# High and low parts of W_in's later pieces and of W_out, and the low part of o, made in halves of 512 columns

## The chip, the cores and the metric

The kernel runs on one core of one Trainium2 chip. The metric is the device time of one execution in microseconds, lower being better. One more execution was taken with the hardware profiler, and all views are of that one. Each engine (TensorE for matmuls, VectorE, ScalarE, GpSimd, and SyncE, which issues most transfers) runs its own instructions in the order in which the program lists them, and waits on semaphores where an instruction needs another engine's result.

## What is computed

One decoder block on 1024 tokens of 1024 features, in float32. An adaptive pre-norm feeds one input projection to 2304 columns. Eight heads of mixer A (window 128, two key heads, a sink logit) and eight heads of mixer B (a mixture of three dilated windows) attend. Each mixer's output is normed, the two are concatenated, and one output projection follows; then come a post-norm, a gate and the residual. The second half is a squared-ReLU MLP of 4096 features with the same frame.

```python
h = rms_norm(x, g_attn_pre) * (1 + sc_a) + sh_a
proj = h @ w_in                                   # 1024 x 2304
...
oa = banded_attention(qa, ka, va, A_WINDOW - 1, sink=sink_a)
ob = dilated_mixture_attention(qb, kb, vb)
mixed = concatenate([rms_norm(oa, g_mix_a), rms_norm(ob, g_mix_b)])
x = x + gt_a * rms_norm(mixed @ w_out, g_attn_post)
h = rms_norm(x, g_mlp_pre) * (1 + sc_m) + sh_m
x = x + gt_m * rms_norm(square(relu(h @ w_up)) @ w_down, g_mlp_post)
```

## The kernel before

**High and low parts.** Matmuls run on a format (fp32r) that keeps fewer bits than float32. To keep the accuracy, an operand is split: ScalarE writes a rounded copy, the high part, and VectorE subtracts it from the original and so writes the low part. A product takes three matmuls: high by high, high by low, low by high. The splitting is the work that the change touches, in three places.

**W_in** (`split_w`, lines 547 to 565) arrives as 18 pieces of 128 by 1024 in a staging ring of three slots. Each piece is split into a tile of a ring of three. ScalarE's `hi` is on line 557, VectorE's `lo` on line 560. The function has a parameter `parts`: pieces 0 to 3, which the first projection unit uses, are split in two parts of 512 columns each; pieces 4 to 17 (lines 1071 to 1073) are split whole. The projection's matmuls are on lines 979 to 983 (`chunk_mm`) and, for values, on lines 1054 to 1056 (`proj_v`).

**W_out** (`load_wo`, from line 1487) is split into eight chunks of 128 by 1024, multiplied by a column of norm gains on the way: ScalarE on line 1514, VectorE on line 1517. The result goes into the tile `hw`, which holds the projection's input until then, so a chunk of W_out must wait until the last projection unit has read two chunks of `hw` (`e_free`).

**o**, attention's output, is read back from memory for each block of 128 tokens (`load_o` in `out_block`). ScalarE's high part is on line 1645, VectorE's low part on line 1649; ScalarE then squares it in place (line 1653), VectorE adds the squares up (1657, 1658), a small matmul and GpSimd (1677) make the norm `rab`, and the products on lines 1698 to 1700 use both parts. For blocks 2 to 7 these tiles have 1024 columns, for blocks 0 and 1 they come as two tiles of 512.

**Attention's small steps** share the engines with all this from about 90 us to 415 us: scores (line 1265 for mixer B, 1319 for A), a masked minimum on VectorE (1283), the exponential on ScalarE (1290), a reciprocal (1293), a scaling on GpSimd (1295), transposes on TensorE (1369 to 1376), the high and low part of the probabilities `ph` (ScalarE 1383, VectorE 1387), and the product with the values (1399 to 1410).

**Who sets the order.** The program is not written out by hand. A list scheduler (`Sched`, lines 197 to 333) holds a queue of steps for each engine, each with a modelled duration, dependencies, ring slots that it takes and gives, and a priority number. It picks, again and again, the step with the earliest possible start; on one engine ties are broken by the lower priority number and then by the earlier made step (line 290). A step that depends on another one is ready a modelled latency after it, 0.14 us between ScalarE, VectorE and themselves (`lat`, line 128). TensorE has streams (projection and MLP are `dense`) among which a list of preferences decides. All instructions are then emitted in the order found. Steps of W_in have priority 0, those of W_out 4, those of o 2, the evacuations of the projection -1, and attention's steps 0 and 1.

The durations in the model are formulas, for instance for VectorE and for ScalarE from on-chip memory:

```python
def t_sb(n):
    return 0.098 + 0.00083 * n
...
def t_dv(n):
    return 0.066 + 0.00104 * n
```

**The MLP** follows from about 480 us to the end: seven products for each of eight half-steps (a scheme with sums and differences of sub-blocks), with its own splitting on lines 1913 to 1922, which the change leaves alone.

## Time and profile before

| what | value |
|---|---|
| three runs, us | 1112.59, 1112.41, 1110.45 |
| median, us | 1112.41 |
| the profiled execution's own time, us | 1111.34 |
| its span, first to last instruction, us | 1109.6 |
| TensorE busy, us | 1091.4 |
| VectorE busy, us | 832.9 |
| ScalarE busy, us | 653.2 |
| GpSimd busy, us | 182.1 |
| mean granted TensorE clock | 0.998 |

A line of the profile's groups reads: source line, engine, operation, tile written and tiles read, shapes, count, then total busy time and mean duration, then the idle time of the engine before these instructions and what ended it. PE is TensorE, PEld its loading of weights, DVE VectorE, ACT ScalarE, POOL GpSimd and SPq SyncE's queue of transfers. In a view in order of time, a line begins with the start and the duration in us. In the chain of waits a line is a piece of the one chain of work that ended last, followed back from the end of the program.

### The profile page before, as it was taken

The numbers are of one execution on the slowest core, as the hardware profiler recorded it, in microseconds if no ns is written. First come the engines' busy times: TensorE is split into PE (matmuls) and PEld (weight loads), VectorE is DVE, ScalarE is ACT, GpSimd is POOL, SyncE is SP. The second block draws the span as 40 slices with busy tenths as digits, with TensorE's granted clock in tenths as the row PEclk, the third lists the DMA queues.
The fourth block names the chain that finished last, engine by engine and source line by source line (L and its number), as shares of the span: only waits on it lengthen the run. The fifth ranks groups of instructions, "written<-read, shape, count | busy, mean of one in ns | idle before, by whom it ended". The sixth has DMA issues, their size and how long they took to land.

```text
span 1109.6 us, 15904 instructions
## 1 busy us (share of the span) xinstructions
PE 1091.4 (98%) x5538; PEld 920.2 (83%) x5538; DVE 832.9 (75%) x1472; ACT 653.2 (59%) x1159; POOL 182.1 (16%) x229
## 2 busy tenths in 40 slices
PE   8999999999999999999999999999999999999997
PEld 7898888888988878888888888888888888888885
DVE  8955777898788877789698653898644996527997
ACT  7745766888877766687675234743145632347544
POOL 3013344555632321110000000000000000000003
PEclk9999999999999999999999999999999999999999
DMA  9866758768636526546841379511578013583006
GB/s 362 288 216 197 208 149 248 205 206 242 169 123 206 155 66 229 190 176 227 333 176 39 114 256 345 167 58 52 193 268 313 18 58 114 190 324 132 1 1 152
DMA packets 97432, 198.65 MB, mean 179 GB/s; under 512 B 8328, under 2 KB 31432, under 8 KB 97352
## 3 DMA queue, kind: packets, MB, share of 16 engines
q1 hardware_dynamic: 96632, 195.43, 52.4%
q0 software_dynamic: 576, 2.10, 1.0%
q8 instruction: 44, 0.72, 0.3%
q14 instruction: 36, 0.29, 0.1%
q10 hardware_dynamic: 144, 0.11, 0.0%
HBM read 155.46 MB, written 42.14 MB: 178 GB/s over the span
## 4 chain that ended last, share of the span: by engine, by line
PE 84%; DVE 8%; ACT 3%; issue 2%; DMA 1%; POOL 1%; SPq 0%; POOLq 0%; DVEq 0%; ACTq 0%
PE mlp_ps L2156 18%; PE mlp_ps L2155 18%; PE mlp_ps L2154 18%; PE s_ps L1265 2%; PE pj L979 2%; PE pj L983 2%; PE pj L981 2%; PE y_ps L1698 2%; PE y_ps L1700 2%; PE y_ps L1699 2%; PE pj L1054 1%; PE pj L1056 1%; PE acc L979 1%; PE pj L1055 1%; PE o_ps L1399 1%
## 5 line engine op out<-in xcount | busy, mean ns | idle before, releaser
L2154 PE MATMUL mlp_ps<-hw 128*128 128x512 f32 x896 | 349.6, 390 | 0.0
L2155 PE MATMUL mlp_ps<-hw 128*128 128x512 f32 x896 | 348.7, 389 | 0.6 <-DVE hw L1919 0.6
L2156 PE MATMUL mlp_ps<-hw 128*128 128x512 f32 x896 | 348.6, 389 | 0.0
L2155 PEld LDWEIGHTS mlp_ps<-hw 128*128 128x128 f32 x896 | 168.2, 188 | 36.4 <-DVE hw L1919 1.0
L2154 PEld LDWEIGHTS mlp_ps<-hw 128*128 128x128 f32 x896 | 168.2, 188 | 35.2 <-issue 0.5
L2156 PEld LDWEIGHTS mlp_ps<-hw 128*128 128x128 f32 x896 | 168.2, 188 | 34.9
L1922 DVE TENSOR_TENSOR hw<-w,hw 128x1024 fp32r<-128x1024 f32 x94 | 111.6, 1220 | 106.7 <-ACT hw L1915 106.5
L1915 ACT CAST hw<-w 128x1024 fp32r<-128x1024 f32 x94 | 95.1, 1048 | 136.8 <-PE mlp_ps L2156 98.2
L2260 POOL TENSOR_TENSOR st<-st,nhalf 128x1 f32<-128x1 f32 x8 | 7.4, 927 | 596.6 <-DVE st L2257 596.5
L1915 ACT CAST hw<-u 128x1024 fp32r<-128x1024 f32 x48 | 48.7, 1051 | 64.6 <-PE mlp_ps L2156 64.6
L1387 DVE TENSOR_TENSOR ph<-pt_ps,ph 128x512 fp32r<-128x512 f32 (+1 forms) x110 | 69.3, 644 | 19.2 <-ACT ph L1383 18.4
L1295 POOL TENSOR_SCALAR p_sb<-p_sb,den 128x128 f32<-128x128 f32 (+3 forms) x64 | 52.6, 826 | 120.2 <-DVE den L1293 97.0
L1383 ACT CAST ph<-pt_ps 128x512 fp32r<-128x512 f32 (+1 forms) x110 | 59.1, 554 | 18.8 <-PE pt_ps L1372 17.3
L1922 DVE TENSOR_TENSOR hw<-u,hw 128x1024 fp32r<-128x1024 f32 x48 | 57.0, 1219 | 16.7 <-ACT hw L1915 16.7
L979 PE MATMUL pj<-hw,w_hl 128*128 128x512 f32 x160 | 68.1, 425 | 0.0
L2212 DVE TENSOR_TENSOR yacc<-yacc,mlp_ps 128x512 f32<-128x512 f32 x96 | 62.5, 682 | 7.1 <-PE mlp_ps L2156 7.0
L983 PE MATMUL pj<-hw,w_hl 128*128 128x512 f32 x160 | 63.2, 395 | 0.0
L981 PE MATMUL pj<-hw,w_hl 128*128 128x512 f32 x160 | 63.0, 393 | 0.0
L1157 POOL TENSOR_TENSOR ada_acc<-ada_acc,wa_st 128x512 f32<-128x512 f32 x42 | 55.0, 1310 | 46.2 <-ACT wa_st L1150 22.4
L1290 ACT ACTIVATE p_sb<-p_sb,mn 128x128 f32<-128x128 f32 (+3 forms) x64 | 49.7, 777 | 21.9 <-DVE mn L1283 20.1
L1265 PE MATMUL s_ps<-kt,qt 128*128 128x512 f32 (+2 forms) x192 | 48.8, 354 | 0.9 <-DVE mn L1283 0.7
L1698 PE MATMUL y_ps<-hw,oh 128*128 128x512 f32 x120 | 48.6, 405 | 1.0 <-DVE mn L1283 0.9
(219 smaller groups left out, 2097.4 us busy)
## 6 DMA issues: line engine op xcount, KB each, us to landing
hw<-s_dram SPq DMA_DIRECT2D x84, 512.0 KB, 4.4
wa_st<-in_w_ada SPq DMA_DIRECT2D x32, 512.0 KB, 5.3
w<-in_w_up SPq DMA_DIRECT2D x32, 512.0 KB, 5.1
w<-in_w_down SPq DMA_DIRECT2D x32, 512.0 KB, 8.3
s_dram<-hw SPq DMA_DIRECT2D x28, 512.0 KB, 4.5
qk_dram<-hl SPq DMA_DIRECT2D x52, 256.0 KB, 3.5
kt<-qk_dram SPq DMA_DIRECT2D x40, 256.0 KB, 5.8
w_st<-in_w_in SPq DMA_DIRECT2D x18, 512.0 KB, 4.4
```

The lines of the kernel that those rows point to most:

```text
L979: T.matmul(ps, wt[:, 0, c0:c0 + P], hw[:, k, 0, t], start=(k == 0), stop=False)
L981: T.matmul(ps, wt[:, 1, c0:c0 + P], hw[:, k, 0, t], start=False, stop=False)
L983: T.matmul(ps, wt[:, 0, c0:c0 + P], hw[:, k, 1, t], start=False, stop=(k == KC - 1))
L1265: T.matmul(s[:, :cw], q_t[u, h, qb // 4][:, qb % 4 * P:qb % 4 * P + P], k_t[u, h, m][:, hl, :cw], start=(hl == 0), stop=(hl == 1))
L1387: V.tensor_tensor(b["ph"][:, 1, :w], b["pt"][:, :w], b["ph"][:, 0, :w].bitcast(F32), ALU.subtract)
L1698: T.matmul(ps[:], oh, wh, start=(k == 4 * i), stop=False)
L1915: A.copy(out[j][0], flat(src[j]))
L1922: V.tensor_tensor(out[j][1], flat(src[j]), out[j][0].bitcast(F32), ALU.subtract)
L2154: T.matmul(ps[m][:], sh, mh, start=starts and k == 0, stop=False, **kw)
L2155: T.matmul(ps[m][:], sh, ml_, start=False, stop=False, **kw)
L2156: T.matmul(ps[m][:], sl, mh, start=False, stop=k == 3, **kw)
L2212: e = op("DVE", t_dv(512), lambda: V.tensor_tensor(y(), y(), ps[m][:], ALU.add), [e, ml.e_y[tb, n]], gives=gives, prio=1)
```

## The change

The loop over the later pieces of W_in asks for two parts. For W_out the two steps of each chunk become two steps for each half of 512 columns: a half waits only for the one chunk of `hw` that it overwrites, the second half's steps come after the first's on each engine, and the staging slot is given back after the last one. The event on which products wait is that of the second half. For o the low part alone is made in halves of four sub-blocks of 128 where the tile has 1024 columns; the squares and the products wait for the last one.

```diff
     for i in range(4, 18):
         load_w(i)
-        split_w(i, prio=0)
+        split_w(i, 2, prio=0)
...
-                def f_h(k=k, g=g, raw=raw):
-                    A.mul(wo_at(k, 0), raw().rearrange("p (n c) -> p n c", n=2), g)
-
-                def f_lo(k=k, g=g, raw=raw):
-                    V.scalar_tensor_tensor(wo_at(k, 1), raw().rearrange("p (n c) -> p n c", n=2), g, wo_at(k, 0).bitcast(F32),
-                                           ALU.mult, ALU.subtract)
-                eh = op("ACT", t_sb(D) + AP_COST, f_h, [es[i]] + [e_free[k // 4][x] for x in (2 * (k % 4), 2 * (k % 4) + 1)],
-                        prio=4)
-                ph2.e_wo[k] = op("DVE", t_dv(D) + AP_DV, f_lo, [eh] + turn + ([last_hl] if k > 3 else []), prio=4,
-                                 gives=[(r_stg, 1)] if j == 1 else [(r_w, 1), (r_wl, 1)] if k == 1 else [])
+                for n in range(2):
+                    def f_h(k=k, n=n, g=g, raw=raw):
+                        A.mul(wo_at(k, 0)[:, n], raw()[:, 512 * n:512 * n + 512], g)
+
+                    def f_lo(k=k, n=n, g=g, raw=raw):
+                        V.scalar_tensor_tensor(wo_at(k, 1)[:, n], raw()[:, 512 * n:512 * n + 512], g,
+                                               wo_at(k, 0)[:, n].bitcast(F32), ALU.mult, ALU.subtract)
+                    eh = op("ACT", t_sb(512) + AP_COST, f_h, [es[i], e_free[k // 4][2 * (k % 4) + n]] + ([eh] if n else []),
+                            prio=4)
+                    ph2.e_wo[k] = op("DVE", t_dv(512) + AP_DV, f_lo,
+                                     [eh] + turn + ([last_hl] if k > 3 else []) + ([ph2.e_wo[k]] if n else []), prio=4,
+                                     gives=[] if not n else [(r_stg, 1)] if j == 1 else [(r_w, 1), (r_wl, 1)] if k == 1
+                                     else [])
...
-            def f_ol():
-                V.tensor_tensor(b["hl", m][1], b["now", m], b["hl", m][0].bitcast(F32), ALU.subtract)
-            eo = op("DVE", t_dv(P * n), f_ol, [eh], prio=2)
+            eo = eh
+            for x in range(max(1, n // 4)):
+                def f_ol(x=slice(4 * x, 4 * x + 4)):
+                    V.tensor_tensor(b["hl", m][1][:, x], b["now", m][:, x], b["hl", m][0][:, x].bitcast(F32), ALU.subtract)
+                eo = op("DVE", t_dv(P * min(n, 4)), f_ol, [eh, eo], prio=2)
```

## The prediction

> **What bounds the kernel now.** I read the page's busy times first, then the table of stretches, then the chain of waits, and last the order of time around the places where TensorE lost time.

> ```profile
> span 1109.6 us, 15904 instructions
> PE 1091.4 (98%) x5538; PEld 920.2 (83%) x5538; DVE 832.9 (75%) x1472; ACT 653.2 (59%) x1159; POOL 182.1 (16%) x229
> ```

> The span and 1.7 us around it make the profiled execution's 1111.34 us; the other three runs have a median of 1112.41, and I take every difference off that median. TensorE is busy for 98% of the span, so a change that leaves its matmuls alone can win only from the 18.2 us in which it idles, and from little delays that its modelled ends hide. The change touches work between 50 and 475 us. The stretches that hold the most of it (from and to, length, then busy time and instructions of TensorE, weight load, VectorE, ScalarE and GpSimd, then clock, DMA share and GB/s):

> ```profile
> 100.00:150.00 50.00, 49.21 (x285) 40.82 (x284) 37.42 (x97) 34.93 (x75) 21.40 (x22) 1.00 0.65 180
> 150.00:200.00 50.00, 49.58 (x289) 42.45 (x287) 38.90 (x98) 33.71 (x66) 21.88 (x22) 1.00 0.66 203
> 200.00:250.00 50.00, 49.65 (x304) 43.00 (x303) 44.90 (x140) 41.50 (x121) 27.12 (x42) 1.00 0.69 203
> 300.00:350.00 50.00, 49.72 (x316) 44.20 (x315) 41.27 (x101) 33.30 (x68) 15.62 (x16) 1.00 0.50 151
> 350.00:400.00 50.00, 48.23 (x298) 41.27 (x297) 39.98 (x113) 37.03 (x79) 16.51 (x20) 1.00 0.47 140
> 400.00:450.00 50.00, 48.64 (x250) 40.22 (x250) 36.70 (x69) 32.17 (x52) 10.40 (x13) 1.00 0.53 175
> ```

> TensorE's idle time in these six is 0.79 + 0.42 + 0.35 + 0.28 + 1.77 + 1.36 = 4.97 us. VectorE is at 73% to 90% and ScalarE at 64% to 83%: on the mean neither is full, yet TensorE waits. What a wait is made of is seen in the chain, where whole low and high parts of weights stand ahead of attention's small steps:

> ```profile
> 99.26 1.14 DVE w_hl L560
> 115.31 1.24 DVE w_hl L560
> 160.55 1.24 DVE w_hl L560
> 227.26 1.14 DVE w_hl L560
> 328.58 1.20 DVE hw L1517
> 350.49 1.77 ACT hw L1514 x2
> 354.07 0.99 ACT hw L1514
> ```

> These lines (start, us, engine and line) are the low part of W_in (L560), the low part of W_out (L1517) and its high part (L1514). Each is followed within a few microseconds, 13 in one case, by a stall of TensorE. In order of time, one matmul row before each stall and one after:

> ```profile
> 102.72 0.38 PE L1399 MATMUL o_ps<-ph,v_hl 128*128 128x256 f32 x1
> 103.45 0.39 PE L1399 MATMUL o_ps<-ph,v_hl 128*128 128x256 f32 x1 [0.34 <-DVE ph L1387]
> ...
> 118.46 0.89 PE L1399 MATMUL o_ps<-ph,v_hl 128*128 128x256 f32 x2
> 119.18 0.40 PE L1404 MATMUL o_ps<-ph,v_hl 128*128 128x256 f32 x2
> ...
> 165.38 0.34 PE L1402 MATMUL o_ps<-ph,v_hl 128*128 128x128 f32 x2
> 165.99 0.97 PE L1265 MATMUL s_ps<-kt,qt 128*128 128x512 f32 x4 [0.28 <-DVE mn L1283]
> ...
> 239.98 0.40 PE L1410 MATMUL o_ps<-ph,va_hl 128*128 128x512 f32 x1
> 240.72 0.51 PE L1410 MATMUL o_ps<-ph,va_hl 128*128 128x512 f32 x1 [0.35 <-DVE ph L1387]
> ...
> 356.62 0.38 PE L1372 MATMUL pt_ps<-head,p_sb 128*128 128x128 f32 x2
> 357.93 0.38 PE L1399 MATMUL o_ps<-ph,v_hl 128*128 128x256 f32 x1 [0.92 <-ACT ph L1383]
> 358.65 0.39 PE L1399 MATMUL o_ps<-ph,v_hl 128*128 128x256 f32 x1 [0.34 <-DVE ph L1387]
> 358.88 0.39 PE L1404 MATMUL o_ps<-ph,v_hl 128*128 128x256 f32 x2
> 359.11 0.53 PE L1399 MATMUL o_ps<-ph,v_hl 128*128 128x256 f32 x2
> ```

> From start to start, two undisturbed matmuls of 256 columns take 0.23 us (358.88 to 359.11), so one takes 0.12, one of 512 twice that and one of 128 half. The rows' own durations are longer because a matmul's end overlaps the next one; an idle time in brackets therefore understates a loss. By starts, TensorE lost 0.73 - 0.12 = 0.61 us at 102.7; 0.72 - 0.23 = 0.49 at 118.5; 0.61 - 0.12 = 0.49 at 165.4; 0.74 - 0.23 = 0.51 at 240; and 0.72 - 0.12 = 0.60 at 357.9, with 0.92 of idle time ahead of it. That is 3.62 us, with a whole high or low part in the chain ahead of each.

> **The change, part by part.** It removes nothing from the arithmetic. It turns 14 whole pieces of W_in, 8 of W_out and 6 low parts of o into two instructions each: 28 more on VectorE (14 + 8 + 6) and 22 more on ScalarE (14 + 8), since o's high part stays whole. Their costs:

> ```profile
> 38.43 0.69 DVE L560 TENSOR_TENSOR w_hl<-w_st,w_hl 128x512 fp32r<-128x512 f32 x1
> 39.03 1.22 DVE L722 TENSOR_TENSOR hw<-xnT,hw 128x1024 fp32r<-128x1024 f32 x1
> ...
> 53.52 1.22 DVE L560 TENSOR_TENSOR w_hl<-w_st,w_hl 128x1024 fp32r<-128x1024 f32 x1
> 54.66 1.22 DVE L722 TENSOR_TENSOR hw<-full,hw 128x1024 fp32r<-128x1024 f32 x1
> ...
> 330.23 2.19 ACT L1514 ACTIVATE hw<-wo_st,head 128x1024 fp32r<-128x1024 f32 x2
> ...
> 103.76 1.33 ACT L1150 ACTIVATE wa_st<-wa_st,cond 128x512 f32<-128x512 f32 x2
> ...
> L1514 ACT ACTIVATE hw<-wo_st,head 128x1024 fp32r<-128x1024 f32 x8 | 9.0, 1156 | 2.6 <-PE pj L981 2.6
> L1150 ACT ACTIVATE wa_st<-wa_st,cond 128x512 f32<-128x512 f32 x42 | 29.6, 721 | 0.2 <-DMA wa_st<-in_w_ada 0.2
> L557 ACT CAST w_hl<-w_st 128x1024 fp32r<-128x1024 f32 x14 | 14.7, 1050 | 6.6 <-PE acc L983 4.0 <-DMA w_st<-in_w_in 1.4 <-PE pj L1056 1.0
> ```

> The first rows are the most useful, as the kernel already makes W_in's first pieces in halves. Durations alone would say 2 x 0.69 - 1.22 = 0.16 us more per piece. But the engine takes its next instruction before the last one's end: a half holds VectorE for 0.60 us (38.43 to 39.03), a whole for 1.14 (53.52 to 54.66). A split costs 0.06 us, and an instruction that is ready behind a weight waits at most 0.60 instead of 1.14: 0.54 less. On ScalarE a whole of W_out holds it for 2.19 - 1.16 = 1.03 us and a scaled half, taken from L1150, for 1.33 - 0.72 = 0.61, so a split costs 0.19 and shortens the queue by 0.42. W_in's casts (1050 ns whole, in the last row) I bound by the same 0.61 and 0.19.

> [...]

> By rows the added work is 28 x 0.06 = 1.7 us on VectorE and at most 22 x 0.19 = 4.2 us on ScalarE, over the 425 us from 50 to 475. I put it at nothing on the path, because the idle shares above hide it; where that cover is gone it is a rival.

> *W_in.* The high half is done after 0.61 us, so VectorE starts 0.44 us sooner. The last low half would end 0.61 + 0.60 + 0.69 = 1.90 us after the first cast starts, against 1.05 + 1.22 = 2.27 now, if nothing comes between: the staging slot, and with it the next load, comes free up to 0.4 us sooner, or later by what overtakes. No stall above is one of a projection matmul, so neither shows.

> *Overtaking.* The order is decided by the planner inside the program. It takes the earliest possible start, then the lower priority number, then the earlier made step. It adds 0.14 us between dependent steps even on one engine, so that after a first half any step that is already ready goes ahead of the second, even where the second half has the better number. On VectorE the second half must wait for the second cast besides. A step of priority 0 that ties with a ready second half of W_in loses, as W_in's steps were made first. W_out (priority 4) loses against all of attention (0 and 1).

> *Sum of the gain.* At the four VectorE places the cap is the smaller of 0.54 and the loss: 0.54 + 0.49 + 0.49 + 0.51 = 2.03. At 357 us three whole copies of W_out stand ahead on ScalarE; 3 x 0.42 = 1.26 of the 1.52 lost there. Upper end 3.3 us. Lower end: nothing, if the second half always follows at once. I take two thirds, 2.2 us, since the planner's 0.14 us lets a ready step past at most of these boundaries, and ties go the other way at some. 1112.4 - 2.2 = 1110.2.

> *W_out's earlier start.* Each half now waits for one chunk of hw to be free, not two. The row of L1514 has 2.6 us of idle that a projection matmul ended. A copy could start there one projection step sooner (three matmuls of 512 columns, 3 x 0.23 = 0.7 us), but no stall above waits for it; I take nothing, with 0.7 either way as the bound.

> *o's low part.* The products and the squares still wait for its last half: 0.06 us later, more if overtaken. That is the first rival.

> **The rivals.** *Slower: o's second half is overtaken.* It has priority 2, below nearly all of VectorE's other steps of that stage. The last block is the place:

> ```profile
> 473.74 1.22 DVE L1649 TENSOR_TENSOR ol<-o_sb,oh 128x1024 fp32r<-128x1024 f32 x1
> ...
> 478.97 1.68 POOL rab L1677
> ...
> 512.24 0.50 PE L2155 MATMUL mlp_ps<-hw 128*128 128x512 f32 x1 [0.55 <-DVE hw L1919]
> ```

> Low part, sum of squares and norm follow each other there, and the chain runs from that norm through ScalarE and VectorE to TensorE's stall at 512. A step of 1024 columns let in between costs 1.14 + 0.06 = 1.2 us, and with no spare time all of it reaches that stall. It decides the sign if it happens in the last block and in two of the five earlier ones without cover while the gain fails: 3 x 1.2 = 3.6, so 1116.0. Against it: in every row of stalls above it is attention that TensorE waits for, never o's low part.

> *No change.* The second halves follow at once, or what they let past is late for another reason; the added 1.7 us lies in idle time or, at worst, on the path: 1112.4 to 1114.1. For it: at 118.5 us the projection's rotation also stands between the weight and the step that TensorE waits for.

> *Faster still.* The planner's new order also mends stalls that I didn't list: up to all 4.97 us of idle time, 1107.4. For it: every later step moves, and VectorE's spare time is there. Against it: a new order makes new stalls as easily.

> That the halves aren't made is not a case: the loops are plain.

> **How the numbers follow.** A measurement of this kernel can tell about 0.2%, 2.2 us, from no change: faster is below 1110.2, slower above 1114.6. The forecast has 0.50 and sits on the bound, so half of it is faster and half the same. Faster still has 0.17, no change 0.15 (all within), slower 0.18. Faster 0.25 + 0.17 = 0.42; same 0.25 + 0.15 = 0.40; slower 0.18. The range takes in the forecast's ends (1109.1 to 1112.4), no change to 1114.1, most of faster still and the lower part of slower: 1107.0 to 1115.0. The likeliest case's own range is 1109.1 to 1112.4.

> **What would show it.** Right: on each of the two engines 28 more rows of 512 columns for W_in's later pieces and 16 for W_out, on VectorE 12 more for o, all of 0.60 to 0.80 us; attention's steps between halves on VectorE; the whole pieces gone from the chain; TensorE's idle time from 100 to 450 us down by a microsecond or more, and fewer waits for ph. Wrong: halves back to back with the stalls at the same steps (no change); a wait for ol or for rab before y_ps, or a longer one at the first MLP products (slower); stalls at quite other steps (the new order, not the halves, decides).

## The result, and the profile after

| what | before | after |
|---|---|---|
| median of six runs, us | 1111.14 | 1116.31 |
| lowest to highest, us | 1110.29 to 1112.59 | 1114.08 to 1120.38 |
| the profiled execution's own time, us | 1111.34 | 1114.08 |
| mean granted TensorE clock of the runs | 0.998 (profiled) | 0.994 to 0.998, mean 0.9963 |

The kernel became slower: the ratio is 1.005, with a 95% interval of 1.0036 to 1.0063, where 1110.2 us and most likely a small gain had been forecast. 1116.31 lies above the range, too. The forecast was counted from the median of the first three runs (1112.41), which is 1.3 us above the median of all six. The top of the page after:

```profile
span 1112.3 us, 15974 instructions
PE 1091.5 (98%) x5538; PEld 920.6 (83%) x5538; DVE 841.0 (76%) x1502; ACT 656.4 (59%) x1181; POOL 181.2 (16%) x227
```

TensorE's work is the same (1091.5 us against 1091.4), so all that was lost is idle time of TensorE or a lower clock. VectorE's busy time rose by 8.1 us. The prediction counted 1.7 us, by the time for which an instruction holds its engine (28 x 0.06), and full durations would make 4.5 (28 x 0.16), so some instructions also became longer. In the table of stretches (columns as in the prediction), first one row of the kernel before that was not shown:

```profile
250.00:300.00 50.00, 50.00 (x356) 46.13 (x355) 41.11 (x146) 43.06 (x123) 29.92 (x47) 1.00 0.77 219
```

Then the kernel after:

```profile
100.00:150.00 50.00, 49.21 (x291) 42.26 (x292) 38.61 (x101) 35.35 (x78) 21.89 (x22) 1.00 0.59 175
150.00:200.00 50.00, 49.28 (x280) 41.21 (x279) 39.74 (x101) 33.42 (x69) 21.69 (x22) 1.00 0.66 202
200.00:250.00 50.00, 49.00 (x297) 42.24 (x296) 43.76 (x141) 39.81 (x119) 27.46 (x41) 1.00 0.67 203
250.00:300.00 50.00, 49.28 (x340) 44.36 (x340) 44.90 (x144) 43.61 (x124) 28.47 (x45) 1.00 0.76 214
300.00:350.00 50.00, 49.52 (x320) 44.48 (x320) 39.33 (x106) 34.35 (x75) 17.16 (x18) 1.00 0.46 141
350.00:400.00 50.00, 46.97 (x286) 39.69 (x285) 44.68 (x124) 39.74 (x84) 15.75 (x19) 1.00 0.51 151
400.00:450.00 50.00, 49.49 (x264) 42.21 (x264) 35.52 (x68) 32.27 (x55) 9.91 (x14) 1.00 0.50 166
```

TensorE's idle time in these seven was 4.97 us before (1.77 of it from 350 to 400) and is 0.79 + 0.72 + 1.00 + 0.72 + 0.48 + 3.03 + 0.51 = 7.25 us. It grew in each stretch from 150 to 400 us and shrank only after that. The groups show the instructions that the change made:

```profile
L560 DVE TENSOR_TENSOR w_hl<-w_st,w_hl 128x512 fp32r<-128x512 f32 x36 | 26.9, 758 | 6.6 <-ACT w_hl L557 6.5
L557 ACT CAST w_hl<-w_st 128x512 fp32r<-128x512 f32 x36 | 21.6, 616 | 7.1 <-PE acc L983 4.0 <-DMA w_st<-in_w_in 1.9 <-PE pj L1056 1.0
L1518 DVE SCALAR_TENSOR_TENSOR hw<-wo_st,head,hw 128x512 fp32r<-128x512 f32 x16 | 11.5, 743 | 0.0
L1654 DVE TENSOR_TENSOR ol<-o_sb,oh 128x512 fp32r<-128x512 f32 x15 | 10.6, 721 | 0.3 <-ACT oh L1648 0.3
```

All halves were made. But a half of W_in on VectorE has a mean of 758 ns where the eight halves of the kernel before had 687. One of them, of 1.69 us, carries 1.0 us of the 2.6 us by which the 36 exceed that mean. In order of time, VectorE, GpSimd and TensorE around 205 us of the kernel after:

```profile
203.53 3.14 POOL L1157 TENSOR_TENSOR ada_acc<-ada_acc,wa_st 128x512 f32<-128x512 f32 x2 [2.68 <-issue]
...
205.53 1.69 DVE L560 TENSOR_TENSOR w_hl<-w_st,w_hl 128x512 fp32r<-128x512 f32 x1
...
207.78 0.28 PE L1399 MATMUL o_ps<-ph,v_hl 128*128 128x256 f32 x1
208.08 1.27 DVE L1387 TENSOR_TENSOR ph<-pt_ps,ph 128x512 fp32r<-128x512 f32 x2
208.81 0.39 PE L1399 MATMUL o_ps<-ph,v_hl 128*128 128x256 f32 x1 [0.74 <-DVE ph L1387]
```

The half takes 1.69 us and ends 0.55 us after GpSimd's additions (207.22 against 206.67), and the following low part of `ph` reaches TensorE 0.91 us late (1.03 from start to start less 0.12). The kernel before has no stall at this place. Two theories came first. **Cost**: more instructions cost time wherever they stand. **Order**: the halves are harmless, and the new order of everything else is worse. A third, **collision**, came out of the first runs: where one of GpSimd's additions and a low part on VectorE run side by side, one of the two takes longer (1.99 us against 1.31, or 1.79 against 0.69, see below), and a gap between halves lets the addition start before the second half.

### The profile page after: what moved, and what is told of

The parts are those of the page before. It is cut to its first block, busy times and chain, and to the rows that moved or that the text cites. A ratio compares the mean times of both kernels' runs of the same rounds, so it can differ in the third digit from the quotient of the medians.

```text
span 1112.3 us, 15974 instructions
## 1 busy us (share of the span) xinstructions
PE 1091.5 (98%) x5538; PEld 920.6 (83%) x5538; DVE 841.0 (76%) x1502; ACT 656.4 (59%) x1181; POOL 181.2 (16%) x227
## 4 chain that ended last, share of the span: by engine, by line
PE 78%; DVE 7%; ACT 3%; issue 1%; DMA 1%; POOL 0%; SPq 0%; POOLq 0%; DVEq 0%; ACTq 0%
PE mlp_ps L2160 18%; PE mlp_ps L2161 18%; PE mlp_ps L2159 18%; PE pj L979 2%; PE pj L983 2%; PE pj L981 2%; PE y_ps L1705 2%; PE y_ps L1703 2%; PE y_ps L1704 2%; PE s_ps L1265 2%; PE o_ps L1399 1%; PE pt_ps L1369 1%; DVE ph L1387 1%; PE s_ps L1319 1%; PE o_ps L1410 1%
## 5 line engine op out<-in xcount | busy, mean ns | idle before, releaser
L1387 DVE TENSOR_TENSOR ph<-pt_ps,ph 128x512 fp32r<-128x512 f32 (+1 forms) x110 | 69.2, 644 | 14.9 <-ACT ph L1383 14.1
L1383 ACT CAST ph<-pt_ps 128x512 fp32r<-128x512 f32 (+1 forms) x110 | 58.7, 555 | 15.3 <-PE pt_ps L1372 13.4
L983 PE MATMUL pj<-hw,w_hl 128*128 128x512 f32 x160 | 63.2, 395 | 0.0
L981 PE MATMUL pj<-hw,w_hl 128*128 128x512 f32 x160 | 62.9, 393 | 0.0
L1265 PE MATMUL s_ps<-kt,qt 128*128 128x512 f32 (+2 forms) x192 | 49.5, 355 | 1.5 <-DVE mn L1283 1.4
```

The costliest lines, as they stand in the source:

```text
L981: T.matmul(ps, wt[:, 1, c0:c0 + P], hw[:, k, 0, t], start=False, stop=False)
L983: T.matmul(ps, wt[:, 0, c0:c0 + P], hw[:, k, 1, t], start=False, stop=(k == KC - 1))
L1265: T.matmul(s[:, :cw], q_t[u, h, qb // 4][:, qb % 4 * P:qb % 4 * P + P], k_t[u, h, m][:, hl, :cw], start=(hl == 0), stop=(hl == 1))
L1387: V.tensor_tensor(b["ph"][:, 1, :w], b["pt"][:, :w], b["ph"][:, 0, :w].bitcast(F32), ALU.subtract)
```

## The experiments

Each run was timed in five rounds against the kernel before on the same chip. Times are medians, and a ratio is to the kernel before. The groups of runs were on different chips, on which the kernel before had medians of 1110.9 to 1111.2 us.

### Halves or order

**Halves, old order.** Each whole step of the kernel before issues its two halves itself, so no order changes on any engine.

```diff
-                A.copy(w_hl[i][:, 0, c], w_raw[i][:, c])
+                for c in cut(c):
+                    A.copy(w_hl[i][:, 0, c], w_raw[i][:, c])
```

(The low part, W_out and o's low part likewise; `cut` gives two slices of 512.)

> The planner is left as it was before (whole steps, same order on all engines), and each of the 28 whole steps issues two instructions of 512 columns one right after the other. Theory 'order' (the new plan, not the instructions, costs the time): within 1 us of before, ratio 0.999 to 1.001. Theory 'cost' (28 more instructions on VectorE and 22 on ScalarE cost it, 1.7 us and up to 4.2 us of engine time): 2 to 5 us slower, ratio 1.002 to 1.0045.

Measured: 1114.31 us (before: 1111.03), ratio 1.0031, 1.0019 to 1.0042. Without any step overtaking another, the halves alone cost 3.3 us. All five stalls that the prediction named are still there, as must be in an order in which nothing can go between two halves.

**Wholes, new order.** The changed program's order, but the first half's step issues nothing and the second half's step the whole.

> The planner makes the new plan with half steps, so all other instructions stand in the order of the changed kernel, but the first half step issues nothing and the second one issues the whole instruction of 1024 columns. Theory 'order': as slow as the changed kernel or slower, ratio 1.003 to 1.007, with the stalls of TensorE at the same steps. Theory 'cost': back at the time of before, ratio 0.999 to 1.001.

Measured: 1117.48 us, ratio 1.0057, 1.0044 to 1.007. The new order costs without halves as well, at least as much as with them, so neither theory holds alone.

**One part alone**, each with its own plan: W_in, W_out (only the diff's lines for that part), and o.

> Only W_in's later pieces in halves, with its own new plan. Theory 'order' (each plan rolls its own stalls): anything from 0.998 to 1.005, and the three parts done alone don't add up to the whole. Theory 'cost': 14 of 28 instructions, so half of the loss, ratio 1.002 to 1.003.

> Only W_out in halves, with its own new plan; W_in and o as before, and up to about 325 us the order should be the same as before. Theory 'order': 0.998 to 1.004, decided by TensorE's idle time from 325 to 420 us alone. Theory 'cost': 8 of 28 instructions on VectorE, ratio about 1.001. Rival of the prediction (o is overtaken): not touched here, so no wait for ol.

> Only o's low part in halves, with its own plan. Its six added instructions have 0.06 us each; W_in alone had 4.4 us and W_out alone 1.3 us over before, and all three together 5.3 us. If the parts add up, o alone is within 1 us of before (1111 us). If a new order costs by itself wherever it comes from, it is 1 to 4 us over before.

Measured: W_in 1115.41 us (ratio 1.0038, 1.0024 to 1.0052), W_out 1112.36 (1.0014, 1.0005 to 1.0023), o 1111.54 (1.0004, 0.9995 to 1.0013). W_in alone loses most (more than the 1.002 to 1.003 that the theory of cost gave it), and o's low part loses nothing that can be measured. As each part has an order of its own, this does not part the halves' cost from the order's.

**Two more orders.** The planner's start cost of a VectorE instruction is changed by 2 ns, in the kernel before and in the changed one:

```diff
 def t_dv(n):
-    return 0.066 + 0.00104 * n
+    return 0.068 + 0.00104 * n
```

> The kernel before, all steps whole, but the planner's start cost of a VectorE instruction 0.068 us where it was 0.066: same instructions, another order on every engine. If an order by chance is some us worse than the one of before: 1113 to 1117 us. If the order hardly matters, and it was the halves' places that cost: within 1 us of before.

> The changed kernel with the planner's start cost of a VectorE instruction 0.068 us where it was 0.066: the same halves in a third order. If the order by chance decides, 1112 to 1119 us, and over 1 us away from the changed kernel's 1116.3 on either side. If halves cost by themselves, within 1 us of the changed kernel.

Measured: whole steps 1120.23 us (1.0072, 1.0058 to 1.0086), above the 1113 to 1117 that were expected, and halves 1116.77 (1.0045, 1.0033 to 1.0057). With the same instructions as before, another order costs 9 us, and with this constant the halves come out 3.5 us better than the wholes. The halves landed only 0.5 us from the changed kernel, so of their expectation the distance of over 1 us failed. Of the three orders tried with whole steps (1111.2, 1117.5 and 1120.2 us) the kernel before has the best, and a change that makes the planner start afresh can lose that.

### Collisions with GpSimd

What happens in the old order is seen at 203 us, where the planner puts W_in's piece 13 and one of GpSimd's additions for the adaptive modulation side by side. The kernel before:

```profile
202.76 1.23 DVE L560 TENSOR_TENSOR w_hl<-w_st,w_hl 128x1024 fp32r<-128x1024 f32 x1
...
203.15 1.99 POOL L1157 TENSOR_TENSOR ada_acc<-ada_acc,wa_st 128x512 f32<-128x512 f32 x1 [1.35 <-ACT wa_st L1150]
```

The whole started first; the addition, which has a mean of 1.31 us, took 1.99 and ended 1.15 us after the whole did. TensorE lost nothing. The same place with halves in the old order (lines 565, 1162 and 1392 are 560, 1157 and 1387 of before):

```profile
202.21 2.40 DVE L565 TENSOR_TENSOR w_hl<-w_st,w_hl 128x512 fp32r<-128x512 f32 x2
...
202.70 1.36 POOL L1162 TENSOR_TENSOR ada_acc<-ada_acc,wa_st 128x512 f32<-128x512 f32 x1 [1.44 <-ACT wa_st L1155]
...
205.35 0.28 PE L1404 MATMUL o_ps<-ph,v_hl 128*128 128x256 f32 x1
...
205.98 1.15 DVE L1392 TENSOR_TENSOR ph<-pt_ps,ph 128x384 fp32r<-128x384 f32 x2
...
206.59 0.39 PE L1404 MATMUL o_ps<-ph,v_hl 128*128 128x256 f32 x1 [0.95 <-DVE ph L1392]
```

Now the addition goes between the halves: it has its usual length, and the second half, which began at 202.82, takes 1.79 us instead of 0.69. The low part of `ph` comes late and TensorE loses 1.24 - 0.12 = 1.12 us. In both pairs the instruction that started first has about its usual length (the whole 1.23 us, the addition 1.36), and the one that started second is longer: 1.99 against 1.31 us for the addition, 1.79 against 0.69 for the half. What in the hardware makes it so is not shown.

**Piece 13 whole**, all else in halves and in the old order:

```diff
-        return [slice(x, x + 512) for x in range(c.start, c.stop, 512)]
+        return [c] if i == 13 else [slice(x, x + 512) for x in range(c.start, c.stop, 512)]
```

> The old order with the twelve whole instructions of W_in's other pieces, W_out's 16 and o's in halves, but piece 13 (the one at 203 us, between whose halves GpSimd's add slipped in) left whole on both engines. Collision theory: the stall of 1.12 us that TensorE had at 205.4 us is gone, its second half's 1.79 us too, and the time is about 1.1 us under that of the old order with all in halves (3.3 us over before): 2.2 us over before, a ratio of about 1.002. Fixed-cost theory (each added instruction costs its start): one piece of 22 changes 0.15 us, so the ratio stays at 1.003.

Measured: 1112.60 us (before: 1110.88), ratio 1.0016, 1.0008 to 1.0025. One piece of 14 gave back half of the loss, 1.7 us; the intervals of this kernel and of the one with all in halves still overlap a little, but in the trace the whole is first again and the stall of 1.12 us is gone: TensorE loses at most 0.36 us at a time from 196 to 240 us. VectorE's and GpSimd's rows:

```profile
203.61 1.23 DVE L565 TENSOR_TENSOR w_hl<-w_st,w_hl 128x1024 fp32r<-128x1024 f32 x1
...
204.00 1.99 POOL L1162 TENSOR_TENSOR ada_acc<-ada_acc,wa_st 128x512 f32<-128x512 f32 x1 [1.34 <-ACT wa_st L1155]
```

**Without the additions**, in the kernel before and in the old order with halves:

```diff
-                    G.tensor_tensor(ada.acc[:, :512], ada.acc[:, :512], parts()[:, j], ALU.add)
+                    pass
```

> The kernel before without GpSimd's 42 adds to the adaptive modulation's accumulator (so those sums are left out). Collision theory: VectorE's stretched instructions between 100 and 400 us lose most of their 2.6 us, and TensorE gains at most 1 us of it: 1110.0 to 1111.0 us. Fixed-cost theory: as before, 1111.0 us. It is the base for the next kernel.

> The old order with all in halves, without GpSimd's 42 adds (those sums are left out). Collision theory: no second half of W_in above 0.75 us near 203 us, no stall of TensorE at 205 us; the difference to the whole steps without the adds is 1.0 to 2.0 us where it was 3.3 us with them. Fixed-cost theory: the difference stays at 3.3 us.

Measured: wholes 1109.62 us (0.999, 0.9982 to 0.9999), a little under what was expected, and halves 1111.29 (1.000, 0.9991 to 1.0009). The halves now cost 1.67 us by the medians where it was 3.3. In the trace of halves without additions, no half near 203 us is late, and TensorE's two products follow each other. VectorE's and TensorE's rows:

```profile
201.90 1.29 DVE L565 TENSOR_TENSOR w_hl<-w_st,w_hl 128x512 fp32r<-128x512 f32 x2
...
205.03 0.52 PE L1404 MATMUL o_ps<-ph,v_hl 128*128 128x256 f32 x2
```

So the collisions are 1.6 to 1.7 us of the 3.3. Piece 13 tells it in the new orders, too. In the four with W_in in halves and with the additions (the changed kernel, W_in alone, the other plan with halves, and a run below) its second half takes 1.69 to 1.70 us, and TensorE loses 0.90 to 0.92 us behind it; in the two without the additions the half takes 0.68 us and TensorE loses nothing there. The other half of the 3.3 stays without any collision and goes with the 50 added instructions. By engine:

**Only VectorE's halves**, in the old order, ScalarE's high parts whole:

> The old order with only VectorE's low parts in halves, ScalarE's high parts whole. Collision theory: nearly all of the 3.3 us is here, since GpSimd's add slips in between VectorE's halves and TensorE's stall at 205 us comes back: 2.3 to 3.3 us over before. Fixed-cost theory, by engine: ScalarE's second starts are 0.1 to 0.19 us each for 22 steps against VectorE's 0.06 us for 28, so VectorE alone has 0.9 to 1.7 us over before.

Measured: 1113.44 us, ratio 1.0022, 1.0013 to 1.0031, with the stall of 1.12 us back (at 206.7). That is 2.6 of the 3.3 us; 0.7 is left for ScalarE's halves, less than the intervals can hold apart.

### What the new order costs on top

**The changed kernel without the additions:**

> The changed kernel (halves in their own new order) without GpSimd's 42 adds (those sums are left out). If the collisions with the adds are nearly all of what the new order costs: within 1 us of the old order in halves without the adds (1111.3), so 1111 to 1112.5, and the stalls of TensorE at 208 us gone. If the new order costs by itself (TensorE's products stand in worse places): 2 us or more over it, 1113.3 or more, 3.5 us or more over the whole steps without the adds (1109.6).

Measured: 1115.45 us, ratio 1.004, 1.0028 to 1.0053. The changed kernel gains little from it, 0.9 us, and stands about 4 us above the old order in halves without the additions. So in the new order most of the loss is not the additions. The trace is of the slowest of the six runs (1119.09 us) and not typical: TensorE lost 2.6 us at 101.6 and 2.0 us at 196.0, both behind a late transfer, and half rate (see below) followed both: the mean granted clock is 0.83 from 100 to 110 us and from 190 to 200.

The first of these shows one place where the new order is worse. The kernel before casts this `ph` on ScalarE while a piece of W_in is still under way (first row). In the changed kernel the cast of the piece's first half stands ahead of it, and `ph` waits for the transfer, too:

```profile
96.30 0.48 ACT L1383 CAST ph<-pt_ps 128x384 fp32r<-128x384 f32 x1
...
98.16 0.62 ACT L557 CAST w_hl<-w_st 128x512 fp32r<-128x512 f32 x1 [1.85 <-DMA w_st<-in_w_in]
98.69 0.47 ACT L1383 CAST ph<-pt_ps 128x384 fp32r<-128x384 f32 x1
```

TensorE then loses 0.68 us at 100.0 and 0.93 at 101.3, where the kernel before lost 0.61 at 102.7. Over all traces the cast that waits for this transfer starts between 97.1 and 100.6 us; why it varies is open. The changed kernel's longest stall, with ScalarE's rows ahead of it:

```profile
377.54 1.28 PE L1265 MATMUL s_ps<-kt,qt 128*128 128x512 f32 x4
...
377.99 0.69 ACT L1720 ACTIVATE y_sb<-y_ps,rab 128x512 f32<-128x512 f32 x1 [0.24 <-DVE den L1293]
...
379.10 0.69 ACT L1720 ACTIVATE y_sb<-y_ps,rab 128x512 f32<-128x512 f32 x1
...
379.69 0.96 ACT L1383 CAST ph<-pt_ps 128x512 fp32r<-128x512 f32 x2
...
380.32 0.38 PE L1399 MATMUL o_ps<-ph,v_hl 128*128 128x256 f32 x1 [1.50 <-ACT ph L1383]
```

TensorE had its transposes done by 377.8, but two evictions of the output projection and a copy stand ahead of the cast that it needs. The same stall is in the trace of W_out alone and, with 1.69 us, in that of whole pieces in the new order, so it comes from the order and not from the pieces' size.

**Evictions behind the cast**: in the changed kernel the first two of them are issued after the next cast of `ph`; nothing else moves. The second kernel leaves out the additions as well.

```diff
             A.copy(b["ph"][:, 0, :w], b["pt"][:, :w])
+            while held_y:
+                held_y.pop()()
```

> The changed kernel with one edit of ScalarE's order: the first two evictions of y (0.69 us each), which stand ahead of a cast of ph while TensorE idles 1.66 us at 378.5 us, follow that cast. If this stall is what the new order costs, by itself and by the clock that it can take down: the stall falls under 0.6 us, the time is 1 to 3 us under the changed kernel's 1116.3 (1113.3 to 1115.3), and the mean granted clock of the runs rises from 0.9963 towards 0.998. If the new order's cost is spread over many places: within 0.7 us of 1116.3.

> The same edit of ScalarE's order in the changed kernel, without GpSimd's 42 adds (those sums are left out). With the adds left out but the old place of the evictions it had 1115.45 us, the old order in halves 1111.3. If that stall and the collisions are what the new order costs: 1111.5 to 1113. If not: 1114.5 to 1115.5.

Measured: 1115.28 us (1.0041, 1.0029 to 1.0053) and 1113.09 (1.0018, 1.0009 to 1.0027). That is 1.0 us under the changed kernel, inside its interval, and 2.4 us under the changed kernel without additions, just above the range that was expected for it. In the trace of the first the stall became two, of 0.93 and 0.79 us, so it did not fall as far as expected, since the second cast came behind the evictions. ScalarE's and TensorE's rows there:

```profile
381.13 0.59 ACT L1384 CAST ph<-pt_ps 128x512 fp32r<-128x512 f32 x1
381.62 1.27 ACT L1724 ACTIVATE y_sb<-y_ps,rab 128x512 f32<-128x512 f32 x2
382.55 0.35 PE L1402 MATMUL o_ps<-ph,v_hl 128*128 128x256 f32 x1 [0.77 <-DVE ot L1442]
382.77 0.49 ACT L1384 CAST ph<-pt_ps 128x384 fp32r<-128x384 f32 x1
...
383.46 0.39 PE L1402 MATMUL o_ps<-ph,v_hl 128*128 128x256 f32 x1 [0.56 <-DVE ph L1390]
```

With the 0.61 us right behind it TensorE lost 2.27 us there before this edit and loses 1.73 after it. So the stall was moved more than removed, its price is not shown by these runs, and the 2.4 us are not explained by it. Without additions 1.8 us above the old order in halves are left.

### What a long stall costs besides

```profile
374.18:377.59 3.41, 1.52 (x7) 1.00 1.01 369
377.59:381.00 3.41, 3.41 (x16) 0.50 0.24 75
```

In the changed kernel the same stall falls across two windows, with 1.06 us of idle time in the first and 0.84 in the second, and nothing follows:

```profile
376.40:379.82 3.42, 2.36 (x17) 1.00 0.86 234
```

The two runs of the other plan tell the same of a wait of 2.05 us for the MLP's first products: inside one window it was followed by half the clock (halves), split into 1.5 and 0.5 us it was not (wholes). Over all traces the seven windows with 1.67 us or more of idle time are each followed by a fall to half the clock, three of the nine with 1.28 to 1.58 us are, and none with less.

**Four stalls put in.** In the kernel before, four casts of `ph` between 265 and 325 us are issued six times instead of once:

```diff
-            A.copy(b["ph"][:, 0, :w], b["pt"][:, :w])
+            n_ph.append(0)
+            for _ in range(6 if len(n_ph) in (56, 63, 69, 75) else 1):
+                A.copy(b["ph"][:, 0, :w], b["pt"][:, :w])
```

> The kernel before with four stalls put in: at four casts of ph by ScalarE between 265 and 325 us the same cast is issued six times (some 2.4 us more at each; nothing else changes). If a stall of TensorE costs its own length and no more: the time rises by the sum of the stalls that the trace shows (some 1.5 to 2.4 us each, 6 to 9.6 us in all), and the granted clock stays at 1.00 after each. If a stall of this length takes the clock down for some us: 10-us windows with a granted clock under 0.9 behind some of the four, products of 128 columns at 213 ns instead of 109 ns, the mean clock at 0.993 to 0.996, and a time 1.5 to 2 us above the stalls' sum for each such window.

Measured: 1124.24 us (before: 1111.05), 13.2 us more, ratio 1.0117, 1.0104 to 1.013; the runs' clocks are 0.995 to 0.997. By starts TensorE lost 2.1, 2.2, 2.8 and 2.7 us at the four places, 9.8 in all, and 3.4 us are more than the stalls' sum. They are found behind the third and the fourth stall. The window behind the third:

```profile
314.30:317.71 3.41, 3.41 (x14) 0.50 0.00 0
```

And TensorE's rows in order of time there:

```profile
310.90 0.28 PE L1057 MATMUL pj<-w_hl,hw 128*128 128x256 f32 x1
313.30 0.50 PE L1413 MATMUL o_ps<-ph,va_hl 128*128 128x512 f32 x1 [2.11 <-ACT ph L1386]
...
314.39 0.41 PE L1055 MATMUL pj<-w_hl,hw 128*128 128x256 f32 x1
314.61 0.41 PE L1056 MATMUL pj<-w_hl,hw 128*128 128x256 f32 x1
...
317.89 0.28 PE L1055 MATMUL pj<-w_hl,hw 128*128 128x256 f32 x1
318.00 0.28 PE L1056 MATMUL pj<-w_hl,hw 128*128 128x256 f32 x1
```

From 314.39 to 317.89 products of 256 columns start 0.21 to 0.22 us apart, then 0.11 again: 3.4 us at half rate, which cost about 1.7 us. Behind the fourth stall (1.32 us and then 0.61 and 0.73) it is the same. Behind the second (1.68 us) nothing of the kind happened; it falls across two windows, with 0.52 and 1.23 us of idle time. The expectation of a clock that falls behind some of the stalls held, sum included.

## Why the prediction was wrong, point by point

**The step that failed: "I put it at nothing on the path".** The added instructions were put at nothing, and so was what a fresh order does to all other steps, as the sum has only the listed stalls in it. The halves cost 3.3 us in the old order, where nothing overtakes anything: 1.6 to 1.7 are collisions, 1.7 are left without them. That this is the 1.7 that the prediction worked out for VectorE alone is luck. Without additions the halves in the old order added 2.5 us to VectorE's busy time (831.0 to 833.5) and 3.0 to ScalarE's (652.8 to 655.8), and the time rose by 1.7. ScalarE's 4.2 was a high bound: by starts a split costs 0.19 there for W_out (in the changed kernel a half holds the engine for 0.614 us, in the kernel before a whole for 1.041), but 0.09 for W_in (0.520 and 0.948). The cover was judged by busy shares over hundreds of microseconds, while TensorE waits for small steps of these two engines one after another; that each start ahead of such a step is paid fits this and is not shown step by step. Neither engine was full (over the span before, VectorE was busy for 75% and ScalarE for 59%), and the kernel lost all the same.

**The reading of the stalls: "with a whole high or low part in the chain ahead of each".** For three of the losses it was wrong. ScalarE's and VectorE's rows of the kernel before at 102.7:

```profile
101.34 0.72 ACT L1150 ACTIVATE wa_st<-wa_st,cond 128x512 f32<-128x512 f32 x1
...
102.08 0.97 ACT L1383 CAST ph<-pt_ps 128x512 fp32r<-128x512 f32 x2
...
102.70 1.15 DVE L1387 TENSOR_TENSOR ph<-pt_ps,ph 128x512 fp32r<-128x512 f32 x2 [0.66 <-ACT ph L1383]
```

VectorE had ended W_in's piece at 100.49 and stood idle for 0.66 us right before the low part that TensorE waited for. So no earlier work of VectorE's made that part late: TensorE's 0.61 us is the time from `ph`'s high part to its low part, behind a scaling of the modulation on ScalarE. The 0.60 us at 357.9 are of the same kind (VectorE idle for 0.31 us until the cast). Before the stall at 240 VectorE was idle for 0.99 us at 235.9, after W_in's piece; this stall goes away with wholes and with halves alike once GpSimd's additions are left out. At 118.5 and 165.4 VectorE, and for the other 0.92 us at 357.9 ScalarE, worked without a gap from the weight's piece to the late step. There the reading may be right, and halves in the old order do not test it.

**What became of the five stalls.** In the changed kernel they are gone: at the same casts of `ph`, counted in order, TensorE loses nothing, nor at the score of 165.4 (there are 0.48 us two products earlier). So the 3.62 us that the prediction counted were won at these places, but others came instead: 0.68 and 0.93 us at 100, 0.48 at 163.4, 0.91 at 208.8, 0.62 at 253.9, 1.66 and 0.61 at 380 and 0.74 at 384, 6.6 us in all. Nor was it the halves' size that won them: with whole pieces in the new order four of the five (not that at 240) are gone, too. TensorE's rows of two stretches, before and then after:

```profile
350.00:362.00 12.00, 10.74 (x70) 1.00 0.55 191
376.00:390.00 14.00, 13.77 (x86) 1.00 0.30 90
...
350.00:362.00 12.00, 12.00 (x74) 1.00 0.73 232
376.00:390.00 14.00, 11.53 (x71) 1.00 0.42 126
```

**The cost that was missing: VectorE and GpSimd.** The prediction looked at GpSimd's instructions only as a queue. The row at 203.15 was in the trace before: an addition of 1.99 us, against a mean of 1.31, beside a whole low part. With the whole it was GpSimd's instruction that took longer, and TensorE lost nothing there; with a gap in the middle it was VectorE's (1.79 us against 0.69), and TensorE lost 1.12 us.

**Overtaking** happened: another instruction stood between the halves on VectorE at 17 of 28 boundaries, near the two thirds that the prediction took. It was right as a count. That it won anything by itself is not shown, as the order without halves loses most of the listed stalls as well.

**The rival "slower"** named the sign and a time, 1116.0, that is near the result by luck, as its mechanism is not what happened: o's low part alone has a ratio of 1.0004. A wait for `ol` before y_ps did appear, 0.6 us at 384, and belongs to one of the tiles of 512 of blocks 0 and 1, which the change left whole. What came true is the last line of the prediction's signs of error: stalls at quite other steps.

**Adding up.** By medians the change costs 5.2 us. Counted from the old order, 3.3 are the halves as such (1.6 to 1.7 collisions, 1.7 left without them) and about 2 the new order with its longer stalls. Counted from the new order, whole pieces cost 6.4 us, and the halves give 1.2 back. So the sum can be parted in more than one way, and the size of either part holds for its order alone. Seen another way, the profiled execution is 2.9 us above the median before, and the runs' median lies another 2.2 above it. Their mean clock of 0.9963 against 0.9981 in 16 later runs of the kernel before would explain 2 us of 1092 busy ones. That the clock fell behind the stall at 378 us in those runs, where it lay inside one window, is argued from its like in other kernels; their traces weren't taken. Open, too, is how much each place of the new order costs in the median: the losses by place are of single executions.

## What to carry to other kernels

Before a long instruction is blamed for a stall, look whether its engine stood idle between it and the step that was late; if so, splitting it cannot mend that stall. Before an instruction is split, look what the other engines do at that moment: here one of GpSimd's additions took 1.99 us instead of 1.31 beside a whole low part on VectorE, and with that low part cut the addition started before the second half, which took 1.79 us instead of 0.69, 1.1 us more. Where a planner makes the order, test an edit in the old order as well as in its own, or its price and the new order's luck come mixed.

## What was not expected of the hardware

A stall of TensorE of about 2 us cost nearly twice its length: behind 2.3 us of idleness at 311 us products ran at half rate for 3.4 us, which cost about 1.7 us more. Whether that follows differed with where the stall lay: the same stall of 1.66 us was followed by half rate in W_out alone, where one window of 3.41 us held all of it, and not in the changed kernel's profile, where two windows shared it with 1.06 and 0.84 us of idle time. Where the limits of the windows lie differs between these two executions: at 374.18 us in the one and 376.40 in the other, 2.22 apart. Nor was a window before a fall idle throughout: it had 1.28 to 2.34 us of idle time, and of the nine windows with 1.28 to 1.58 us six were followed by nothing.
